# All pairs of a hybrid decoder layer's output projection by seven products

## The chip, the cores and the metric

The kernel runs on one core of a Trainium2 chip. The metric is the device time of one execution in microseconds (us); lower is better. A core has five engines that run side by side and meet at semaphores: TensorE (PE, matmuls into PSUM; its weight loads are shown as PEld), VectorE (DVE), ScalarE (ACT), GpSimd (POOL) and SyncE (SP), which here only issues DMAs. Each engine takes its instructions in order. A kernel's time is the median of several runs; one more execution was recorded by the hardware profiler, and all rows quoted here are of that one.

## The reference

One step of a decoder layer: a norm, a combined input projection, three groups of heads, and one output projection of width 1024.

```python
def _layer(x, conv_buf, buf_k, buf_v, mem_k, mem_v, ...):
    h = _rmsnorm(x, g_pre)
    z = h @ w_in                       # 1024 -> 2816 columns
    cb, cc, ch, cg, q, k, v, ag, mq, mg = _split_cols(z)
    out_a = silu(cg) * cb * conv3(cc * ch)              # 256 features
    out_b = silu(ag) * sliding_window_attention(q, k, v, sinks, window=128)   # 512
    out_c = silu(mg) * attention(mq, mem_k, mem_v)      # 256
    y = jnp.concatenate([out_a, out_b, out_c], axis=-1) @ w_out   # 1024 -> 1024
    return x + _rmsnorm(y, g_post), ...
```

It is computed for a prompt of 4096 tokens and for 8 sequences of 8 new tokens (the sample, 64 rows), in float32.

## The kernel before

**Precision and products.** Every float32 operand of a large matmul is split into a high and a low part in a reduced type (fp32r); a product is the sum of three matmuls, hi x hi, lo x hi and hi x lo. The split is one copy on ScalarE and one subtraction on VectorE. A 2 x 2 block product can be made from seven block products instead of eight, from sums and differences of the blocks of both operands. The input projection is made in this way but for the first two blocks of phase one.

**Stages.** `input_projection` runs through three phases over groups of columns of w_in. Each phase has eight blocks of 520 tokens, and each block seven products (eight plain ones in those two). Phase two (`ph == 1`) ends with q, k and v written to DRAM. Phase three has fewer columns, and carries the memory keys and the attention of the first 256 tokens beside it. Then comes the third stage, which the change is about: the attention and the output projection, 16 pairs of 128-token blocks.

**The output projection.** Blocks 0 to 5 (pairs 0 to 2) are plain: `Block.split` parts the gated features ("mix"), and `Block.run` makes two halves of 512 columns of eight k-tiles each, line 1639. From pair 3 on (`PLAIN_PAIRS = 3`) `Pair.run` makes a 2 x 2 block product: the two token blocks against the two halves of the columns, over feature tiles 0 to 3 only (two k-tiles per block of features). Feature tiles 4 to 7 are added with plain matmuls into the same PSUM banks. All its matmuls are made in the inner `product`, line 1750, one k-tile at a time; before each k-tile it calls what the list `starts` has for that step. A pair has 30 steps. Products with new=True begin a bank, others accumulate on it. The sums of features are made by GpSimd (`sums_of`, line 1695), their parts by ScalarE and VectorE (`lows`, lines 1678 and 1681). The five sums of weights are made by VectorE (`weight_sum`) during the plain pairs. All weight tiles stay in SBUF: pool `wa` has 21 slots of 4 KB a partition, pool `wt` six. A bank is read in parts: L1785 copies c12 to s3, L1787 adds c21 to s3 into s4, L1790 and L1793 subtract c12 and c21 from s4, L1759 copies a finished half, L1770 adds the last.

The order of the products before, with the number of k-tiles, is: c12 by a11 x T3 (2), c21 by a22 x T4 (2), c12 by rows0 x b22 (2), c21 by rows1 x b11 (2), then plain (8), c11 by diag x T1 (2), plain (2), c11 by down1 x T7 (2), plain (4), c22 by down0 x T6 (2), plain (4).

**Attention.** It runs one half (128 queries) at a time, ahead of the projection, in pieces that are hung on steps of the pair. `first_half` has transposes of the memory probabilities (L1368), window scores (L1333), and the products of the half before with the values (L1390, L1396, L1059); VectorE and ScalarE then mask, reduce and exponentiate (L1342, L1343, L1281, L1289), and the gates (L1255, L1407) multiply the results into mix. `memory_half` makes memory scores (L1355), `second_half` the window transposes (L1378) and the loads for the half after next. In a pair, the odd half's three pieces stand at steps 12, 16 and 19, the even half's at 24, 27 and 32, which is step 2 of the next pair.

**Who sets the order.** TensorE's order in the third stage is the program's (`manual_schedule`). Other engines' instructions are ordered by the scheduler from expected times, except those in `keep_in_program_order`. SP's DMAs are issued in such an order too, and one that waits holds all behind it. PSUM: two banks "z" for the projection, three pairs of banks for the attention.

Of the kernel before, what the change touches and what calls it, by code (L numbers as in the profile page):

```python
# [47 lines left out]
def f(ap):  # L48
    return ap.bitcast(F32)
# [3 lines left out]
def hybrid_layer(ctx: ExitStack, tc: tile.TileContext, a: dict):  # L53
# [834 lines left out]
    wo, wo_raw = [[None, None] for _ in range(KT)], {}  # L888

    def wo_load(j):  # L890
        h, k = divmod(j, KT)
        if 10 <= j < 14:

            if j % 2 == 0:
                third["raw"] = hxp.tile([P, KH, HW], F32, tag="hx", name=f"wor{j}").rearrange("p k n -> p (k n)")
            wo_raw[j] = third["raw"][:, 512 * (j % 2) : 512 * (j % 2) + 512]
        else:
            wo_raw[j] = third["work"].tile([P, 512], F32, tag="u", name=f"wor{j}")
        DMA.dma_start(wo_raw[j], a["w_out"][k][:, 512 * h : 512 * h + 512])

    def wo_split(j):
        h, k = divmod(j, KT)
        wo[k][h] = wa.tile([P, 2, 512], F32R, tag="w", name=f"wo{k}_{h}")
        w_split(wo[k][h], wo_raw.pop(j))
# [16 lines left out]
    def input_projection():  # L921
        for i, (ph, b, p) in enumerate(steps):
# [32 lines left out]
            if i > 0 and steps[i - 1][0] == 1 and steps[i - 1][1] == NBLK - 1:  # L955

                o = PRODUCTS[steps[i - 1][2]][0]
                for q in range(len(PHASES[2])):
# [5 lines left out]
                    else:  # L964
                        jobs.append(load)
                        pending.setdefault(i + 1, []).append(fill)
            if ph == 2 and b == last:
                for j in ((0, 1, 2), (3, 4), (5, 6, 7), (8, 9, 10, 11), (12, 13, 14, 15), (), ())[p]:
                    jobs.append(lambda j=j: wo_load(j))
                    pending.setdefault(i + (3 if j in (10, 11) else 2), []).append(lambda j=j: wo_split(j))  # L970
                if p == 1:
                    pending.setdefault(i + 1, []).append(gains_load)
                if p == 4:
                    jobs.append(blocks[0].split)
# [36 lines left out]
    def open_attention():  # L1011
# [14 lines left out]
        bp = {"k": att.enter_context(tc.tile_pool(name="keys", bufs=1)), "vT": att.enter_context(tc.tile_pool(name="vT", bufs=1))}  # L1026
# [41 lines left out]
    class Chunk:  # L1068


        def __init__(self, c):
            self.c, self.rds, self.q, self.ks = c, {}, [None, None], [None, None]
            self.t0 = NS + CT * c
            self.ts = slice(self.t0, self.t0 + CT)
# [6 lines left out]
        def load_all_keys(self):  # L1081

            self.kst = third["pre"].tile([P, 4, P + CT], F32R, tag="k", name="kst0")
# [581 lines left out]
    class Pair:  # L1665


        def __init__(self, c):
            self.c = c
# [461 lines left out]
```

## Time and profile before

| | |
|---|---|
| runs, median (lowest to highest) | 1519.56 us (1518.1 to 1525.04) |
| profiled execution, span | 1517.9 us |
| PE, DVE, ACT, POOL busy | 1500.6, 1199.3, 842.7, 392.7 us |
| matmuls, all | 11497 |
| first and last matmul of the plain blocks | 928.7 and 1042.6 us |
| matmuls of `Pair.run` | from 1042.8 us |
| DMA, whole span | 319.71 MB, mean 211 GB/s |

The profiled execution's own span is the time against which sums are made. Matmuls are pipelined: the duration of one includes the way through the array, so durations overlap, and the distance between two starts says what one costs. A row of groups gives a line, an engine, an operation, the tiles written and read, shapes, a count, and busy time and mean duration; behind the second bar stands idle time before it and what ended that. A row of the timeline begins with its start and its duration. In a row of waits stand total, number and longest.

### The profile page before, as it was taken

What the parts mean: (1) busy time and instruction counts of PE and PEld (TensorE: products, weight loads), DVE (VectorE), ACT (ScalarE), POOL (GpSimd) and SP (SyncE); (2) the same over time, 40 slices, a digit from 0 to 9 for tenths busy, and PEclk for the clock granted to TensorE, in tenths of its full rate; (3) what the DMA queues carried; (4) which work ended last, traced back from release to release, by engine and by line L of the source; (5) the groups of instructions that cost most, each with busy time, mean ns of one, the idle gap of its engine ahead of it and who ended that gap; (6) DMA issues with size and microseconds to landing.
All of it is one profiled execution on the core that took longest, in us unless ns stands there. A gap on an engine that the chain in (4) does not pass through costs nothing.

```text
span 1517.9 us, 30946 instructions
## 1 busy us (share of the span) xinstructions
PE 1500.6 (99%) x11497; PEld 1378.7 (91%) x11497; DVE 1199.3 (79%) x2089; ACT 842.7 (56%) x2066; POOL 392.7 (26%) x576
## 2 busy tenths in 40 slices
PE   9999999999999999999999999999999999999997
PEld 9999999999999999999999999788888788877875
DVE  6779888899988777897777768777877788878874
ACT  6676666475322222354454536666666666666652
POOL 0223222211300000000201301234455544455641
PEclk9999999999999999999999999999999999999999
DMA  9999999878855333578786697989755565666552
GB/s 258 157 265 221 289 294 271 264 246 298 211 183 183 128 116 125 180 235 292 227 265 238 208 307 252 282 238 238 201 168 157 160 164 162 176 174 169 153 201 70
DMA packets 217323, 319.71 MB, mean 211 GB/s; under 512 B 37398, under 2 KB 143382, under 8 KB 217142
## 3 DMA queue, kind: packets, MB, share of 16 engines
q1 hardware_dynamic: 196837, 273.54, 61.1%
q0 software_dynamic: 19616, 43.15, 10.5%
q8 instruction: 91, 1.49, 0.4%
q10 hardware_dynamic: 720, 1.05, 0.2%
q14 instruction: 59, 0.48, 0.1%
HBM read 208.50 MB, written 110.15 MB: 210 GB/s over the span
## 4 chain that ended last, share of the span: by engine, by line
PE 79%; DVE 8%; DMA 5%; ACT 4%; issue 2%; SPq 1%; POOL 0%; ACTq 0%; DVEq 0%; POOLq 0%
PE c L368 53%; PE y_c L1750 12%; PE y L1639 2%; PE ws L1333 2%; PE xt L1368 2%; ACT xp L1180 1%; DVE xr L1660 1%; DMA place<-in_xt 1%; PE wo L1059 1%; PE wo L1396 1%; DVE xmx L1169 1%; PE xs L1355 1%; DMA wr_3A<-in_w_in 1%; PE wt L1378 1%; DMA kst<-qd 1%
## 5 line engine op out<-in xcount | busy, mean ns | idle before, releaser
L375 DVE TENSOR_TENSOR z<-c,z 128x520 f32<-128x520 f32 (+1 forms) x308 | 194.3, 644 | 83.7 <-PE c L368 82.7
L1750 PE MATMUL y_c<-wo,pw 128*128 128x512 f32 (+1 forms) x636 | 158.9, 392 | 0.0
L1289 ACT ACTIVATE sm<-sm,wnm 128x128 f32<-128x128 f32 x256 | 99.4, 389 | 72.1 <-DVE wnm L1283 72.1
L1750 PEld LDWEIGHTS y_c<-wo,pw 128*128 128x128 f32 x636 | 114.0, 188 | 27.1 <-issue 3.7
L1192 POOL TENSOR_SCALAR xp<-xp,xrd 128x256 f32<-128x256 f32 x128 | 71.5, 575 | 191.2 <-DVE xrd L1186 186.7
L1180 ACT ACTIVATE xp<-xs,xnm 128x256 f32<-128x256 f32 x128 | 59.1, 473 | 31.5 <-DVE xnm L1170 22.9
L737 POOL CAST wmask<-negs 128x256 uint8<-128x256 f32 x1 | 1.2, 1162 | 266.7 <-DMA negs<-in_wmask 266.7
L1639 PE MATMUL y<-wo,mh 128*128 128x512 f32 x192 | 64.5, 398 | 0.2 <-ACT y L1648 0.2
L1312 POOL TENSOR_SCALAR_AFFINE_SELECT wpv<-wpt 128x512 f32<-128x512 f32 x62 | 56.8, 938 | 8.7 <-ACT wpt L1307 8.5
L1315 POOL TENSOR_SCALAR_AFFINE_SELECT wpt<-wpt 128x512 f32<-128x512 f32 x64 | 46.0, 737 | 38.6 <-ACT wpt L1307 38.2
L1333 PE MATMUL ws<-kst,q 128*128 128x256 f32 (+1 forms) x480 | 55.7, 297 | 0.0
L1343 DVE COPY_PREDICATED sm<-wmask,ws 128x512 f32<-128x512 uint8 x60 | 40.5, 729 | 19.0 <-ACT sm L1342 19.0
L1660 DVE SCALAR_TENSOR_TENSOR xr<-yn,yst,xr 128x1024 f32<-128x1024 f32 (+2 forms) x35 | 51.6, 1479 | 4.6 <-POOL yst L1655 4.5
L407 ACT CAST zh<-z 128x520 fp32r<-128x520 f32 x56 | 33.3, 624 | 35.3 <-DVE z L375 31.9
L276 ACT ACTIVATE nat<-nat 104x1024 f32<-104x1024 f32 x40 | 42.2, 1056 | 18.3 <-DMA nat<-in_x_p 18.3
L377 ACT COPY z<-c 128x520 f32<-128x520 f32 (+1 forms) x44 | 24.4, 554 | 49.3 <-PE c L368 45.0
L1333 PEld LDWEIGHTS ws<-kst,q 128*128 128x128 f32 (+1 forms) x480 | 46.4, 187 | 4.1
L1289 ACT ACTIVATION_READ_ACCUMULATOR sm<-sm,wnm 128x1 f32 x256 | 47.9, 187 | 0.0
L1297 DVE TENSOR_TENSOR sm<-sm,wrd 128x512 f32<-128x512 f32 x64 | 44.5, 695 | 1.1
L1750 PE MATMUL y_c<-wo,pc 128*128 128x512 f32 (+1 forms) x162 | 45.1, 400 | 0.0
L164 POOL DMA_DIRECT2D md<-th x48 | 26.2, 547 | 72.0 <-DVE th L425 59.5
L1639 PEld LDWEIGHTS y<-wo,mh 128*128 128x128 f32 x192 | 36.1, 188 | 8.9 <-issue 1.0
(1037 smaller groups left out, 5538.8 us busy)
## 6 DMA issues: line engine op xcount, KB each, us to landing
q<-qd SPq DMA_DIRECT2D x168, 128.0 KB
xr<-in_x_p SPq DMA_DIRECT2D x32, 512.0 KB
nat<-in_x_p SPq DMA_DIRECT2D x39, 416.0 KB
o_yp<-xr SPq DMA_DIRECT2D x31, 512.0 KB
kst<-qd SPq DMA_DIRECT2D x112, 128.0 KB
md<-th POOLq DMA_DIRECT2D x48, 260.0 KB, 6.4
qd<-zh SPq DMA_DIRECT2D x48, 260.0 KB
qd<-z SPq DMA_DIRECT2D x48, 260.0 KB
```

The costliest lines, as they stand in the source:

```text
L368: TE.matmul(bank[:, :HW], l, r, start=first and i == 0, stop=last and i == 3 * KH - 1)
L375: add = lambda dst, other: V.tensor_tensor(dst, c, other, op=ALU.add)
L1180: S.activation(p[:, i, :], s[:, i, :], AF.Exp, bias=nm[:, i : i + 1], scale=SCALE, accum_out=den[:, i : i + 1])
L1192: G.tensor_scalar(p[:, i, :], p[:, i, :], self.rds[h][:, i : i + 1], 0.5, op0=ALU.mult, op1=ALU.mult)
L1289: S.activation(sm[:, hh, :], sm[:, hh, :], AF.Exp, bias=nm[:, hh : hh + 1], scale=SCALE, accum_out=den[:, hh : hh + 1])
L1297: V.tensor_tensor(sm, sm, rd.unsqueeze(2).to_broadcast([P, 4, P]), op=ALU.mult)
L1312: G.affine_select(pv.rearrange("p (h q) -> p h q", h=4), p3, pattern=[[0, 4], [-1, P]], compare_op=ALU.is_gt, fill=0.0, base=0, channel_mu ...
L1315: G.affine_select(p3, p3, pattern=[[0, 4], [1, P]], compare_op=ALU.is_ge, fill=0.0, base=0, channel_multiplier=-1)
L1333: TE.matmul(out(kvh, col, bank), q(kvh, col, bank)[r], k(kvh, part)[r], start=first, stop=True, skip_group_check=not first, **place)
L1639: TE.matmul(acc, self.hl[l][:, k], wo[k][p][:, r], start=k + i == 0, stop=k + i == KT + 1)
L1660: x = V.scalar_tensor_tensor(self.xr[:m, cs], yn[:m, cs], st[:m, 3:4], self.xr[:m, cs], op0=ALU.mult, op1=ALU.add)
L1750: TE.matmul(acc, a[:, l, k], w[:, r, cs], start=first, stop=k == len(ws) - 1 and i == 2, skip_group_check=not new)
```

## The change

- All 16 pairs are made by `Pair.run`, and all eight feature tiles go into the 2 x 2 product: four k-tiles per product, seven products, 28 steps. `Block.split` and `Block.run` stay for the sample alone.
- The order becomes: c12 by a11 x T3, c12 by rows0 x b22, c21 by a22 x T4, c21 by rows1 x b11, c11 by diag x T1, c22 by down0 x T6, c11 by down1 x T7. In the last pair T7 stands before T6, and T6 is made in two halves of 256 columns after the sample.
- Weights: seven operands of four k-tiles. 21 of these tiles are made in phase two, blocks 1 to 6: raw tiles are loaded, GpSimd adds and subtracts, ScalarE copies, and the parts go to DRAM on GpSimd's queue. b22 and three tiles of b11 are split in phase three as before.
- 22 weight tiles stay in SBUF, and six (`STREAMED`: the fourth tile of each operand but b22) are loaded again in each pair, on SP's queue.
- Every operand of features takes one slot of `wa`: a11, rows0, a22, rows1, diag, down0, down1. They and the reloaded tiles share five slots; a slot is used for about ten steps.
- Keys: each half loads 128 tokens into a ring of three blocks, instead of 256 into a tile of its own.
- Places: the odd half's pieces at 11, 14, 18, the even half's at 22, 25 and 32 (step 4 of the next pair).

```diff
+    G0, G1 = (0, 1, 4, 5), (2, 3, 6, 7)
+    OUT_SUMS = {"T1": ((G1, 0), (G0, 1)), "T3": ((G1, 1), (G0, 1)), "T4": ((G0, 0), (G1, 0)), "T6": ((G1, 0), (G1, 1)),
+                "T7": ((G0, 0), (G0, 1)), "b11": ((G1, 0),), "b22": ((G0, 1),)}
+    STREAMED = (("T3", 3), ("T4", 3), ("b11", 3), ("T1", 3), ("T6", 3), ("T7", 3))
...
+    def out_sum(o, j):
+        x, y = out_raw.pop((o, j))
+        if o in WALKED:
+            G.tensor_tensor(x, x, y, op=ALU.subtract if o in ("T3", "T4") else ALU.add)
+        hi, lo = y.bitcast(F32R), x.bitcast(F32R)
+        S.copy(hi, x)
+        G.tensor_tensor(lo, x, f(hi), op=ALU.subtract)
+        G.dma_start(f(td[o, j][:, 0]), f(hi))
+        G.dma_start(f(td[o, j][:, 1]), f(lo))
+
+    out_sums_at = [(1, b, p) for b in range(1, NBLK - 1) for p in ((5, 6) if b < 4 else (1, 2, 3, 4, 5))]
...
+    def out_load(o, j, pool=None):
+        t = wo[o][j] = (pool or wa).tile([P, 2, 512], F32R, tag="w", name=f"wo{o}_{j}")
+        DMA.dma_start(f(t), f(td[o, j]))
...
-        wt = att.enter_context(tc.tile_pool(name="wt", bufs=6))
+        wt = att.enter_context(tc.tile_pool(name="wt", bufs=7))
...
         def load_keys(self, i):
...
+            at = (2 * self.c + i + 1) % 3 * P
+            self.fill_keys(G if self.c == 1 else DMA, third["ring"][:, :, at : at + P], self.t0 + i * P, P)
...
+        def lows(self, name, src):
+            self.ops[name] = t = wa.tile([P, 2, 512], F32R, tag="w", name=f"{name}{self.c}").rearrange("p a (b n) -> p a b n", n=P)
+            hi, lo = (t[:, i].rearrange("p (a c) n -> p a c n", a=2) for i in range(2))
+            S.copy(hi, src)
+            V.tensor_tensor(lo, src, f(hi), op=ALU.subtract)
...
+        def sum(self, name, x, y, op, raw=None):
+            def fn():
+                t = raw() if raw else sums["sum"].tile([P, 512], F32, tag="sum", name=f"r{name}{self.c}")
+                self.raws[name] = t = t.rearrange("p (a c n) -> p a c n", a=2, c=2)
+                G.tensor_tensor(t, self.part(*x), self.part(*y), op=op)
+            return fn
...
         def run(self, starts, sample=lambda: None):
...
+            def product(acc, name, o, new, cs=left_):
+                for j in range(4):
                     if cs.start == 0:
                         starts.get(at[0], lambda: None)()
                         at[0] += 1
+                    a_, w = self.ops[name], wo[o][j]
                     for i, (l, r) in enumerate(((0, 0), (1, 0), (0, 1))):
+                        TE.matmul(acc, a_[:, l, j], w[:, r, cs], start=new and j + i == 0, stop=j == 3 and i == 2, skip_group_check=not new)
...
+            c12 = psum("z", f"y{c}_c12")
+            product(c12, "a11", "T3", True)
+            tc.keep_in_program_order(S.copy(s3, c12))
+            product(c12, "rows0", "b22", False)
+            S.copy(half(0, 1), c12)
+            c21 = psum("z", f"y{c}_c21")
+            product(c21, "a22", "T4", True)
             V.tensor_tensor(s4, s3, c21, op=ALU.add)
+            V.tensor_tensor(half(0, 0), s4, c12, op=ALU.subtract)
+            product(c21, "rows1", "b11", False)
+            V.tensor_tensor(s3, s4, c21, op=ALU.subtract)
+            S.copy(half(1, 0), c21)
...
             c11 = psum("z", f"y{c}_c11")
+            product(c11, "diag", "T1", True)
             V.tensor_tensor(s3, s3, c11, op=ALU.add)
...
             if not last:
                 c22 = psum("z", f"y{c}_c22")
+                product(c22, "down0", "T6", True)
+                V.tensor_tensor(half(1, 1), c22, s3, op=ALU.add)
...
+                product(c11, "down1", "T7", False)
+                V.tensor_tensor(half(0, 0), c11, half(0, 0), op=ALU.add)
...
+    STEPS = 28
+    pairs = {c: Pair(c) for c in range(NCH)}
+    start_of = lambda c: STEPS * c
...
+    turns = lambda first, odd, even: {2: first} | {h: start_of((h - 3) // 2) + (odd if h % 2 else even) for h in range(3, 2 * NCH + 1)}
+    first_at, memory_at, second_at = turns(0, 11, 22), turns(3, 14, 25), turns(8, 18, STEPS + 4)
...
+    OP_AT = {"a11": (None, -7), "rows0": (-8, -3), "a22": (None, 1), "rows1": (0, 5), "diag": (6, 9), "down0": (8, 13), "down1": (11, 17)}
+    LOAD_AT = {"T3": -3, "T4": 1, "b11": 5, "T1": 13, "T6": 17, "T7": 21}
     for c, p in pairs.items():
         e = start_of(c)
+        for o, n in LOAD_AT.items():
+            if e + n > 0 and (o, c) != ("T4", 0):
+                at(e + n, lambda o=o: out_load(o, 3))
+        for name, (n, m) in OP_AT.items():
+            if c == 0 and name in ("a11", "rows0", "a22"):
+                continue
+            if n is not None:
+                at(e + n, lambda p=p, name=name: p.jobs()[name][0]())
+            at(e + m, lambda p=p, name=name: p.jobs()[name][1]())
...
+        if c > 0:
+            at(e + 3, lambda: left.pop(0)(True))
+            at(e + 6, lambda: left.pop(0)(True))
```

A pair of numbers in `OP_AT` is the step of GpSimd's sum and that of the split, counted from the pair's first step. `left` holds the ends of finished blocks: the addition to the input rows on VectorE (L1660) and the store on SP (L1663).

More of the change, by code (lines that the diff above doesn't have):

```diff
@@ L1780, in ends @@
                 left.append(lambda queued: b.finish(y[n], st[n], a["o_yp"][b.b * P : (b.b + 1) * P, :], queued, last and n == 1))
-            plain = lambda col, ks: [wo[k][col] for k in ks]
-            c12, c21 = psum("z", f"y{c}_c12"), psum("z", f"y{c}_c21")
-            product(c12, self.a11, t["T3"], True)
-            S.copy(s3, c12)
-            product(c21, self.a22, t["T4"], True)
-            V.tensor_tensor(s4, s3, c21, op=ALU.add)
-            product(c12, self.rows[0], b22, False)
```

380 lines of the change are left out of this document (124 added, 256 removed).

## The prediction

> **What bounds the kernel now.** I read the head of the page first, then busy time by stage, then the output projection's matmuls, then one stretch of the timeline around them.
>
> ```profile
> span 1517.9 us, 30946 instructions
> PE 1500.6 (99%) x11497; PEld 1378.7 (91%) x11497; DVE 1199.3 (79%) x2089; ACT 842.7 (56%) x2066; POOL 392.7 (26%) x576
> PEclk9999999999999999999999999999999999999999
> ...
> 300.00:400.00 100.00, 100.00 (x843) 99.83 (x842) 95.23 (x125) 61.07 (x105) 27.07 (x39) 1.00 0.81 243
> 500.00:600.00 100.00, 100.00 (x845) 100.00 (x844) 79.31 (x108) 28.65 (x34) 0.00 (x0) 1.00 0.38 132
> ...
> 929.00:1043.00 114.00, 112.84 (x751) 91.95 (x750) 87.97 (x208) 74.46 (x254) 37.97 (x59) 1.00 0.94 264
> 1043.00:1468.00 425.00, 422.92 (x2827) 340.07 (x2827) 337.80 (x757) 284.51 (x968) 212.46 (x290) 1.00 0.62 171
> ```
>
> A window row gives its length, then busy time of PE, PEld, DVE, ACT and POOL, the granted clock, the DMA share and GB/s. The last two rows are the third stage: 929 to 1043 the three plain pairs, 1043 to 1468 the pairs by products up to the last. PE is full in every row (422.92 of 425.0), at full clock, and DVE is next (337.80, 79%). So the time is PE's work plus PE's waits, and the question is how much of each the change takes and makes.
>
> **Matmuls removed.** These rows count those of the output projection.
>
> ```profile
> L1639 PE MATMUL y<-wo,mh x192: 387/389/501, 928.7 to 1042.6; 128*128 128x512 f32 x192
> ...
> L1639 PE MATMUL y<-wo,ml x96: 387/389/398, 929.0 to 1042.4; 128*128 128x512 f32 x96
> ...
> L1750 PE MATMUL y_c<-wo,pw x636: 279/389/504, 1049.8 to 1507.9; 128*128 128x512 f32 x153, 128*128 128x256 f32 x6
> ...
> L1750 PE MATMUL y_c<-wtT,pd x78: 387/389/398, 1059.2 to 1483.3; 128*128 128x512 f32 x78
> ```
>
> Six plain blocks have 288 (192 + 96), 96 a pair. A pair by products has 14 k-tiles in seven products and 16 plain ones, three matmuls each: 90. After the change every pair has seven products of four k-tiles: 84. That is 3 x 12 + 13 x 6 = 114 matmuls of 512 columns fewer. The 389 ns are not their price, since they overlap. The timeline gives it (start, duration, engine, line, count):
>
> ```profile
> 1253.18 2.25 PE L1750 MATMUL y_c<-wo,pw 128*128 128x512 f32 x9
> ...
> 1255.26 1.53 PE L1750 MATMUL y_c<-wtT,pa 128*128 128x512 f32 x6
> ...
> 1256.63 1.03 PE L1378 MATMUL wt<-ident,sm 128*128 128x128 f32 x8
> ...
> 1257.64 1.64 PE L1750 MATMUL y_c<-wtT,pa 128*128 128x512 f32 x6
> ...
> 1258.69 0.59 ACT L1785 COPY s<-y_c 128x512 f32<-128x512 f32 x1
> ...
> 1259.34 3.08 PE L1750 MATMUL y_c<-wo,pr 128*128 128x512 f32 x12
> ...
> 1262.26 2.98 PE L1750 MATMUL y_c<-wo,pw 128*128 128x512 f32 x12
> ...
> 1265.27 0.59 ACT L1759 COPY yn<-y_c 128x512 f32<-128x512 f32 x1 [3.33 <-PE y_c L1750]
> ```
>
> Nine in a row take 2.25, twelve 2.98 us; less the last one's 0.39 over the steps between starts that is 0.2325 and 0.235. At 0.233 the 114 are worth **-26.6 us**. This is the whole gain, 1.7% and not the 3% that 114 x 0.39 would suggest.
>
> **Waits that go.** Of the two runs "pa" the first goes into c12 and the second into c21; "pr" then goes on in c12, once ScalarE has copied c12 out (L1785, ending 1259.28). From 1257.64 six matmuls need 1.40, so "pr" could start at 1259.04 and starts at 1259.34: a wait of 0.30 a pair, 13 x 0.30 = -3.9 us. The plain stage's waits (114.0 - 112.84 = 1.2) I count as gone for 1.
>
> **Waits that come.** In the new order both sums of one bank follow each other: T3 then b22 into c12, T4 then b11 into c21, and the first must be read out before the second accumulates on it. Two boundaries of a pair's 28 steps (three matmuls, 0.70 us each) so lose the cover that the other bank's product gave.
>
> Step 4, c12: the even half's window transposes stand there now (second_half at STEPS + 4), eight of 1.03 us and two more. A reader starts when the last matmul has ended (1262.26 + 2.98 = 1265.24, copy at 1265.27) and takes 0.59: so the bank is free 0.16 + 0.03 + 0.59 + 0.06 = 0.84 after the nominal next start, under 1.03: the lower end is nothing. But ScalarE was late before too (a11's run ended at 1256.79, its copy began at 1258.69, 1.9 later, behind the memory exponentials); now that product ends later against them. If it were as late again, the wait would be 0.84 + 1.9 - 1.3 = 1.4, the upper end. I take the 0.30 of today, 16 x 0.30 = +4.8.
>
> Step 12, c21: nothing of the attention stands there. first_half of the odd half is at step 11, ahead of a22's last three matmuls. Today it stands at step 12, and the rows show what VectorE has in its queue just then:
>
> ```profile
> 1265.87 1.85 PE L1333 MATMUL ws<-kst,q 128*128 128x256 f32 x16
> ...
> 1267.70 1.07 ACT L1342 COPY sm<-ws 128x512 f32<-128x512 f32 x2
> ...
> 1267.82 0.69 DVE L1681 TENSOR_TENSOR pc<-yn,pc 128x512 fp32r<-128x512 f32 x1 [1.83 <-ACT pc L1678]
> ...
> 1268.43 1.34 DVE L1343 COPY_PREDICATED sm<-wmask,ws 128x512 f32<-128x512 uint8 x2
> ...
> 1269.15 1.04 PE L1059 MATMUL wo<-xp,mkv 128*64 128x128 f32 x16
> ...
> 1269.67 1.26 DVE L1281 TENSOR_REDUCE wmx<-sm 128x4 f32<-128x512 f32 x2
> ...
> 1270.13 1.66 PE L1750 MATMUL y_c<-wo,pw 128*128 128x512 f32 x6
> ...
> 1270.92 0.68 DVE L1255 TENSOR_TENSOR place<-place,wo 128x512 f32<-128x512 f32 x1
> ...
> 1271.66 0.41 DVE L1407 TENSOR_TENSOR place<-place,wo 128x256 f32<-128x256 f32 x1
> ```
>
> The projection resumes at 1270.13. Three matmuls on, at 1270.83, PE wants to write c21 again. The last of them starts at 1270.60 and ends at 1270.99, so s4 = s3 + c21 can start at 1271.02. VectorE, though, serves masks, maxima and both gates (L1255, L1407) first: they are ready earlier and earlier in the program. They end at 1272.07; then the add (0.68, as L1255) and a release of 0.06 (1259.28 to 1259.34): PE goes on at 1272.81, 1.98 late. The subtraction at 1267.82 will have gone, which lets the masks start up to 0.19 sooner, when the first score copy has ended (1267.70 + 1.07/2 = 1268.24 against 1268.43). So 1.8 to 2.0, and I take **1.9 us**. Lower end: the add ahead of the gates, 1271.02 + 0.68 + 0.06 - 1270.83 = 0.93. Upper end: a subtraction of 0.9 (rows below) in front as well, 2.8. Of these 1.9 follows the order that the rows show. It hits the 15 pairs that hold an odd half, and 0.93 the last pair, where no half runs: 15 x 1.9 + 0.9 = **+29.4 us**. Behind the waiting matmul all of PE is queued.
>
> **Work that is hidden.** For five of seven operands GpSimd now makes a raw sum of 512 columns, and ScalarE and VectorE split seven tiles instead of 5.5.
>
> ```profile
> L1695 POOL TENSOR_TENSOR yn<-place 128x512 f32<-128x512 f32 x6 | 8.7, 1457 | 0.0
> ...
> L1681 DVE TENSOR_TENSOR pw<-place,pw 128x512 fp32r<-128x512 f32 x12 | 10.8, 903 | 0.5
> ...
> L1776 DVE TENSOR_TENSOR yn<-yn,gpost 128x512 f32<-128x512 f32 x11 | 12.7, 1154 | 0.0
> ...
> L1770 DVE TENSOR_TENSOR yn<-y_c,s 128x512 f32<-128x512 f32 x12 | 8.2, 683 | 0.0
> ...
> L1678 ACT CAST pw<-place 128x512 fp32r<-128x512 f32 x12 | 8.1, 671 | 0.0
> ```
>
> Per pair: VectorE 1.5 x 0.90 = 1.4, ScalarE 1.5 x 0.67 = 1.0, GpSimd 2.5 x 1.46 = 3.6 us. Over the 12 pairs of 1043 to 1468 they now have 28.2, 23.7 and 17.7 of 35.4, so 29.6, 24.7 and 21.3 of some 36: no engine overtakes PE, and the price is nothing except in VectorE's queue at step 12. Two inputs in SBUF are slow beside GpSimd's work (1154 and 903 ns against 683 with one input in PSUM); the add on c21 is of the second kind.
>
> The Trainium skill ("SBUF — State Buffer", section "Who interferes with whom") says that a VectorE instruction with two SBUF inputs and a GpSimd instruction that reads SBUF block each other. The rows agree. By the page, all 3.6 us of new sums could be lost to VectorE, 33 of 36 us a pair, still under PE, so the sum stays.
>
> Phase two: 21 weight tiles at two GpSimd operations (1.46), one copy, two raw loads and two stores. GpSimd sleeps there (0.00 in 500 to 600) and DMA has 0.38; a block of 336 matmuls takes 40 us (845 in 100), and five tiles of 1 MB in it add some 125 GB/s. PE stayed at 100.00 with VectorE at 95.23 and DMA at 0.81 (300 to 400). Price nothing; without that cover, 42 GpSimd operations that each stretch a VectorE instruction by up to 0.47 (1154 - 683 ns) would be 20 us. The 16 splits of weights at the end of phase three fall to seven, off the path.
>
> Reloads: 6 x 512 KB a pair, less 512 KB for keys that are no longer read twice: 171 GB/s x 35.4 us = 6.1 MB becomes 8.7, 240 GB/s. At 171/0.62 = 276 GB/s per full share that is 0.87; the plain stage ran at 0.94 with 1.2 us of PE's waits. Nothing again, if each load is in time (rivals).
>
> **The sum**: -26.6 - 3.9 - 1.0 + 4.8 + 29.4 = +2.7 us on the profiled span: 1520.6. The runs' median of 1519.56 is 1.7 above the span, so **1522 us**.
>
> **Rivals.** (a) The scheduler puts the add ahead of the gates, wait 0.93: the step costs 16 x 0.93 = 14.9 in place of 29.4, **1507**. For: VectorE's order is not written out. Against: the gates are ready 0.8 us sooner. (b) No wait worth the name at either boundary, only the matmuls go: 1519.56 - 26.6 - 4.9 = **1488**. Against: the bank cannot be read and accumulated at once. (c) Diag's subtraction, which waits for a later GpSimd sum, stands ahead of the add: wait 2.8, 15 x 0.9 more, **1535**. For: GpSimd gets 3.6 us more work, and the sum for diag is queued behind the window masks. (d) The slower one: the fourth T3 tile comes late. Its slot is free when T6 ends (step 23) and its matmul is at step 3: seven steps and the memory scores, 4.9 + 1.1 = 6.0 us. SP issues in order, and stores stand in its way:
>
> ```profile
> SPq L1663 <- DVE xr L1660: 48.2, 12, 12.3
> ```
>
> Such a store holds SP 4.0 us on average. Behind one, with 1.9 us for 512 KB at 276 GB/s, its issue and a queue of other loads, the load lands after 6.0 us from there on; 1 to 2 us a pair more, **1537 to 1552**. Against: today's stores are not at that step. (e) The change does its work but phase two gives back 3 of those 20 us: 1525.
>
> **Chances.** Forecast (1517 to 1526) 0.34, (a) 0.22, (b) 0.13, (c) 0.12, (d) 0.16, (e) 0.03. A measurement of this kernel can tell 0.5% (7.6 us) from no change. Faster by more: (a) and (b), 0.35; within: the forecast and most of (e), 0.36; slower: (c), (d) and the rest, 0.29. From 1500 to 1540 leaves out (b) and the upper half of (d), 0.2. The likeliest case alone spans 1517 to 1526.
>
> **What would show it.** Per pair: 84 projection matmuls; PE idle at the start of b11's product, put down to VectorE's add on c21, near 1.9 us (0.9 in (a), 2.8 in (c)); 0 to 1.4 at b22's start, put down to ScalarE's copy; no wait of PE for a load of wo (else (d)); a pair's period near 36 us against 35.34 now (the next "pa" run after 1255.26 starts at 1290.60). Phase two should still show PE at 100. I am wrong if PE does not wait at step 12, or if it waits for weights.
>
> ```profile
> 1290.60 1.53 PE L1750 MATMUL y_c<-wtT,pa 128*128 128x512 f32 x6
> ```

## The result and the profile after

The kernel after takes **1637.2 us** (median of 4 runs, 1635.6 to 1640.2) against 1522.3 of the kernel before (4 runs, 1518.1 to 1525.4): a ratio of 1.076, 95% interval 1.073 to 1.079. I had forecast 1522, with a range from 1500 to 1540. The head of its page:

```profile
span 1634.9 us, 31287 instructions
...
PE 1536.2 (94%) x11377; PEld 1387.8 (85%) x11377; DVE 1236.4 (76%) x2090; ACT 866.3 (53%) x2092; POOL 554.6 (34%) x690
...
PEclk9999999999999999999999989999999999999997
```

TensorE has 120 matmuls fewer (108 of 512 columns and 12 of 256, worth the 114 of the prediction) and yet is busy 36 us longer, and the span grew by 117.0 us. Both together mean idle time and a slower clock. The windows say where (length, busy time of PE, PEld, DVE, ACT and POOL, granted clock, DMA share, GB/s):

```profile
500.00:600.00 100.00, 95.59 (x774) 94.57 (x773) 76.93 (x100) 32.62 (x44) 38.78 (x43) 0.97 0.62 219
943.00:1078.00 135.00, 114.91 (x701) 89.61 (x700) 88.58 (x201) 78.02 (x263) 57.57 (x70) 0.92 0.84 244
1078.00:1569.00 491.00, 440.80 (x2752) 341.05 (x2751) 358.74 (x756) 294.80 (x965) 262.60 (x302) 0.96 0.73 210
1569.00:1635.00 66.00, 47.97 (x238) 34.42 (x236) 31.43 (x71) 19.21 (x51) 14.65 (x18) 0.80 0.45 156
```

Phase two no longer keeps PE at 100, and in every part of the third stage PE idles and the clock is below 1. Measured from the first matmul of the output projection and the first of each pair:

| part | before, us | after, us | more |
|---|---|---|---|
| up to the first output matmul | 928.7 | 943.0 | 14.2 |
| first three pairs | 114.1 | 135.0 | 20.9 |
| next twelve pairs | 424.6 (35.38 each) | 491.5 (40.96 each) | 66.9 |
| last pair, sample block, ends | 50.5 | 65.4 | 15.0 |
| span | 1517.9 | 1634.9 | 117.0 |

Of the first row's 14.2 us, 11.7 arise in phase two: the input projection ends at 940.6 instead of 928.9, and the whole delay is there by 702. The rest is the window scores that now stand ahead of the first output matmul (1.9 us, and 0.5 of wait).

What PE waited for, summed over the run (engine, line, releaser; us, times, longest):

```profile
PE wo L1423 <- ACT xp L1402: 39.1, 13, 3.3
PE y_c L1742 <- DVE s L1765: 11.0, 12, 1.0
PE y_c L1742 <- ACT s L1760: 6.7, 12, 4.9
...
PE y_c L1742 <- ACT rows L1689: 3.6, 1, 3.6
```

The second row is the wait at step 12 that I had made the main cost: about 1 us a pair, not 1.9. The first row is a wait that I had not foreseen. L1423 is the odd half's products, L1402 ScalarE's copy of the transposed shares out of the one pair of banks "x" that the products need. The timeline of one pair:

```profile
1209.33 2.20 POOL L1342 TENSOR_SCALAR_AFFINE_SELECT wpv<-wpt 128x512 f32<-128x512 f32 x2
...
1209.95 1.04 PE L1401 MATMUL xt<-ident,xp 128*128 128x128 f32 x8
1210.74 1.86 PE L1365 MATMUL ws<-ring,q 128*128 128x256 f32 x16
...
1211.48 1.22 POOL L1345 TENSOR_SCALAR_AFFINE_SELECT wpt<-wpt 128x512 f32<-128x512 f32 x2
...
1212.67 1.26 POOL L1699 TENSOR_TENSOR rdiag<-place 128x512 f32<-128x512 f32 x1
1213.89 1.26 POOL L1699 TENSOR_TENSOR yn<-place 128x512 f32<-128x512 f32 x1
1213.97 0.62 ACT L1689 CAST diag<-rdiag 128x512 fp32r<-128x512 f32 x1 [5.27 <-POOL rdiag L1699]
1214.49 1.01 ACT L1402 COPY xp<-xt 128x1024 f32<-128x1024 f32 x1
...
1215.64 0.69 PE L1423 MATMUL wo<-wpv,vt 64*64 64x256 f32 x2 [3.04 <-ACT xp L1402]
```

Read it from the bottom. PE had its window scores issued by 1212.6 and idled 3.04 us for the copy L1402. The transposes that it copies ended at 1211.0, so the copy could have run then; but ScalarE takes its queue in order, and ahead of the copy stood the cast of diag, which had idled ScalarE for 5.27 us waiting for GpSimd's sum. That sum is a new one, and it stood behind the window masks (L1342, L1345), which end at 1212.7. The same masks are needed by the products, so without the cast PE would have gone on at about 1212.8.

The windows around that wait show a second loss:

```profile
1208.00:1212.60 4.60, 4.60 (x34) 3.87 (x32) 1.68 (x2) 0.59 (x1) 4.60 (x7) 1.00 0.88 275
1212.60:1215.60 3.00, 0.01 (x2) 0.00 (x0) 0.98 (x1) 1.63 (x3) 2.55 (x3) 1.00 0.70 237
1215.60:1219.10 3.50, 3.46 (x24) 1.98 (x26) 2.88 (x8) 1.34 (x5) 1.27 (x1) 0.51 0.77 184
1219.10:1220.70 1.60, 1.59 (x16) 0.94 (x13) 0.85 (x3) 1.33 (x9) 0.00 (x0) 1.00 0.85 262
```

After 3 us without a matmul the granted clock is half of full for 3.41 us (the record runs from 1215.65), which does 1.7 us less work. A twelfth of the regular stretch is such a window: one a pair, 12 x 3.413 = 40.96 us apart.

So a regular pair stands thus, in us: six matmuls fewer -1.40; the wait at step 4 0.32 for the 0.30 that went; step 12 +1.07; the odd half's products +3.1; the clock +1.7; the even half's products, whose masks come late, +0.8. That is +5.3 of the 5.57 measured; the rest is spread over starts of transposes. The 1.7 of the clock is worked out from its record and not from a run of its own.

### The profile page after: what moved, and what is told of

It reads as the page before. It is cut to its first block, busy times and chain, and to the rows that moved or that the text cites. A ratio compares the mean times of both kernels' runs of the same rounds, so it can differ in the third digit from the quotient of the medians.

```text
span 1634.9 us, 31287 instructions
## 1 busy us (share of the span) xinstructions
PE 1536.2 (94%) x11377; PEld 1387.8 (85%) x11377; DVE 1236.4 (76%) x2090; ACT 866.3 (53%) x2092; POOL 554.6 (34%) x690
## 4 chain that ended last, share of the span: by engine, by line
PE 66%; DVE 11%; POOL 10%; DMA 5%; issue 3%; ACT 3%; SPq 1%; DVEq 0%; ACTq 0%; POOLq 0%
PE c L368 43%; PE y_c L1742 9%; POOL xp L1222 3%; PE wo L1429 3%; PE wo L1423 2%; PE wo L1091 2%; POOL wpv L1342 2%; PE ws L1365 1%; POOL rdiag L1699 1%; DVE z L375 1%; DMA os1T<-in_w_out 1%; PE xs L1388 1%; DMA woT<-tdT 1%; POOL yn L1752 1%; POOL wpt L1345 1%
## 5 line engine op out<-in xcount | busy, mean ns | idle before, releaser
L1742 PE MATMUL y_c<-wob,rows 128*128 128x512 f32 x384 | 104.3, 416 | 22.1 <-DVE s L1765 11.0
L1742 PEld LDWEIGHTS y_c<-wob,rows 128*128 128x128 f32 x384 | 72.3, 198 | 45.9 <-DVE s L1765 16.4
L1742 PE MATMUL y_c<-woT,a 128*128 128x512 f32 x384 | 100.8, 404 | 6.5 <-DVE a L1690 3.7
L1742 PE MATMUL y_c<-woT,down 128*128 128x512 f32 (+1 forms) x396 | 100.7, 396 | 0.6 <-DVE down L1690 0.3
L1742 PEld LDWEIGHTS y_c<-woT,a 128*128 128x128 f32 x384 | 72.3, 192 | 24.5 <-DVE a L1690 4.5
L1742 PEld LDWEIGHTS y_c<-woT,down 128*128 128x128 f32 x396 | 71.4, 191 | 18.2 <-issue 3.0
L909 POOL TENSOR_TENSOR os0T<-os0T,os1T 128x512 f32<-128x512 f32 x20 | 25.9, 1297 | 133.1 <-DMA os1T<-in_w_out 131.2
L1210 ACT ACTIVATE xp<-xs,xnm 128x256 f32<-128x256 f32 x128 | 58.9, 471 | 19.3 <-DVE xnm L1200 18.5
L1423 PE MATMUL wo<-wpv,vt 64*64 64x256 f32 x120 | 25.1, 498 | 42.5 <-ACT xp L1402 39.1
L1342 POOL TENSOR_SCALAR_AFFINE_SELECT wpv<-wpt 128x512 f32<-128x512 f32 x62 | 56.7, 935 | 13.3 <-ACT wpt L1337 13.3
L1365 PE MATMUL ws<-ring,q 128*128 128x256 f32 (+1 forms) x480 | 55.9, 298 | 0.5 <-DVE z L375 0.5
L1742 PE MATMUL y_c<-woT,diag 128*128 128x512 f32 x192 | 51.4, 403 | 0.0
L1365 PEld LDWEIGHTS ws<-ring,q 128*128 128x128 f32 (+1 forms) x480 | 46.5, 187 | 4.8 <-DVE z L375 0.7
```

The source lines that it names most:

```text
L1210: S.activation(p[:, i, :], s[:, i, :], AF.Exp, bias=nm[:, i : i + 1], scale=SCALE, accum_out=den[:, i : i + 1])
L1342: G.affine_select(pv.rearrange("p (h q) -> p h q", h=4), p3, pattern=[[0, 4], [-1, P]], compare_op=ALU.is_gt, fill=0.0, base=0, channel_mu ...
L1365: TE.matmul(out(kvh, col, bank), q(kvh, col, bank)[r], k(kvh, part)[r], start=first, stop=True, skip_group_check=not first, **place)
L1423: TE.matmul(o[cs, 1 - n], v[rs, cs], p3[rs, :, 64 - 64 * n : 128 - 64 * n], start=True, stop=False, tile_position=(64 - 64 * n, 64 * kvh))
L1742: TE.matmul(acc, a_[:, l, j], w[:, r, cs], start=new and j + i == 0, stop=j == 3 and i == 2, skip_group_check=not new)
```

## The experiments

My theory after this reading: the sums that GpSimd now makes are late, and the casts that wait for them hold ScalarE's queue in front of copies that PE needs. The rivals: GpSimd is overloaded whoever waits for it; the bank waits at steps 4 and 12 are the loss; the reloads are; phase two is a matter of its own. Each time below is of one execution beside one of the kernel before, which took 1519 to 1525 us. "Period" is the time from the first T3 matmul of a pair to that of the next, in the middle of the third stage.

### The cast of diag behind the copy

```
-    OP_AT = {... "diag": (6, 9), ...}
+    OP_AT = {... "diag": (6, 13), ...}
```

> The kernel after, with one number changed: the split of the diagonal sum (ScalarE's cast and VectorE's subtraction) is issued at step 13 of a pair instead of step 9, so that in ScalarE's order it stands behind the copy of the odd half's transposes instead of ahead of it. GpSimd's own order and load hardly change. Theory (ScalarE's queue is held by a cast that waits for a late GpSimd sum): the 3.0 to 3.3 us in which TensorE waits at the odd half's products shrink to under 0.6, since the masks end at about the time the window scores end; the half-clock window of each pair goes with it; the pair period falls from 41.0 to about 36, the time by 14 x 5.0 = 70 to about 1567 us. Rival (GpSimd is simply too loaded, whoever waits for it): the wait moves to the masks or to the diagonal product and the period stays above 39.5, time over 1615. Rival (the waits at the accumulating banks are the loss): no change, 1630 to 1640.

1597.3 us, period 37.4 (37.8 on the mean of the twelve pairs). PE's waits between 1000 and 1500 us:

```profile
PE y_c L1742 <- DVE s L1765: 15.4, 12, 1.4
PE y_c L1742 <- ACT yn L1769: 5.2, 12, 0.5
PE y_c L1742 <- ACT s L1760: 4.7, 12, 0.6
```

The wait at the products is gone, and between 989 and 1541 us no half-clock window is left. GpSimd's load and order are nearly unchanged, so ScalarE's queue is what it was. But I had expected 1567: the pair gained 3.1 us on the mean and not 5.0, since three bank waits grew as PE came earlier (step 12 to 1.3 idle), and the first pair got longer, from 53.3 to 57.5.

### No sums at all

```
-                t = raw() if raw else sums["sum"].tile(...)
-                self.raws[name] = t = t.rearrange(...)
-                G.tensor_tensor(t, self.part(*x), self.part(*y), op=op)
+                self.raws[name] = self.part(*x)
```

> The kernel after without the five GpSimd sums of a pair: each sum's first term stands for the sum (the output isn't the reference's), while the casts stand in ScalarE's order where they stood, diag's ahead of the transposes' copy. Theory (the cast holds the queue only because GpSimd's sum is late): the wait at the odd half's products and the half-clock windows go, and with them the late masks of the even half; the waits at steps 4 and 12 stay; period about 36.5 or less, time 1575 or less. Rival (the added casts and subtractions load ScalarE and VectorE too much whatever GpSimd does): period 38 or more, time over 1590.

1563.1 us, period 36.3, as the theory had it but for one point: the even half's masks stay late. The 64-row products (L1423) still take 1.9 us a pair, against 1.2 in the kernel before, so the sums aren't the cause of that term. ScalarE's order is that of the kernel after, the cast of diag ahead of the copy; it only has nothing to wait for.

```profile
PE y_c L1740 <- DVE s L1763: 17.6, 13, 1.8
PE y_c L1740 <- ACT s L1758: 2.1, 12, 0.4
```

Of the waits that come back in every pair only the two at the banks are left, the one at step 12 now 1.35 us idle on average, 1.6 from start to start. The difference of the spans, 1634.9 - 1561.4 = **73.5 us, is what the five sums of a pair cost** in this order, of 117.0 in all.

### No reloads

```
     def out_load(o, j, pool=None):
+        if j == 3:
+            wo[o][3] = wo[o][2]
+            return
```

> The kernel after without the fourth tile of six of the seven weight matrices: wherever the fourth tile of a matrix would be used, its third is used again, so that none is loaded in a pair (the output isn't the reference's). Theory (the reloads are in time and cost nothing): 1632 to 1640 us, period 41.0. Rival (the six loads of a pair take the queues or the memory from others, or TensorE waits for them): period under 40, time 1620 or less.

1658.0 us: slower by 20, though the third stage now moves some 120 instead of 210 GB/s. Neither theory nor rival had this. The timeline of ScalarE says why:

```profile
1269.61 0.62 ACT L1692 CAST down<-yn 128x512 fp32r<-128x512 f32 x1 [5.14 <-POOL yn L1702]
1270.13 0.61 ACT L1692 CAST down<-rdown 128x512 fp32r<-128x512 f32 x1
1270.65 1.00 ACT L1405 COPY xp<-xt 128x1024 f32<-128x1024 f32 x1
```

Without the loads to wait for, the scheduler put both casts of "down" ahead of the copy as well, and with them two more sums behind the masks. PE's wait grew to 5.6 us on average (67.3 us in 12 pairs) and the half-clock window to 6.83. A change that touches no cast moved the time by moving casts, so this run doesn't give the price of the reloads. In the kernel after PE waits only 0.3 us for them in all. But two stretches got shorter without them: the first pair took 44.3 us instead of 53.3, and the last with the ends 52.1 instead of 65.4. Whether that is the loads, the slots that they share with the operands, or again the order of the casts, no run shows.

### The bank waits

The odd half at step 12 instead of 11, so that it stands between the two products on c21:

```
-    first_at, memory_at, second_at = turns(0, 11, 22), turns(3, 14, 25), ...
+    first_at, memory_at, second_at = turns(0, 12, 22), turns(3, 15, 25), ...
```

> The kernel after, with the odd half's first part at step 12 instead of 11 and its memory part at 15 instead of 14, so that the half stands between the last matmul of c21's first product and the product that accumulates on it; VectorE's read of c21 then has the half as its cover. Theory: the 1.07 us wait at step 12 goes; the wait at the odd half's products shortens by the one step (0.7 us) by which the half comes later and stays at about 2.4, still long enough for a half-clock window; period about 39.2, time about 1612 us. Rival (the bank wait is the main loss and the clock with it): period near 37, time 1580 or less. Rival (VectorE reaches the read only behind the half's masks and maxima, as forecast): a wait near 1 us remains, 1625 to 1635.

1647.3 us. The waits at steps 4 and 12 went (1.1 us left in 12 pairs), but the casts still held the copy, and now longer: 3.4 us a pair at the products. And the memory transposes (L1401) now waited for GpSimd, 1.25 us a pair.

```profile
PE wo L1423 <- ACT xp L1402: 41.1, 12, 3.7
PE xt L1401 <- POOL xp L1222: 15.0, 22, 1.1
...
1224.15 0.62 ACT L1689 CAST diag<-rdiag 128x512 fp32r<-128x512 f32 x1 [3.57 <-POOL rdiag L1699]
...
1225.83 0.43 PE L1423 MATMUL wo<-wpv,vt 64*64 64x256 f32 x2 [3.63 <-ACT xp L1402]
```

Taking the bank waits away thus gains nothing while the casts hold the copy. The later split of diag and the half at 12 together, with the three casts pinned behind the copy (a pinned instruction keeps its place in program order among the pinned ones):

> The kernel after with the casts of diag, down0 and down1 kept behind the copy of the odd half's transposes (split of diag at step 13, casts pinned), and the odd half at step 12 with its memory part at 15, the order of the products as in the kernel after. Against the run with the later split alone (1597 us, period 37.5) and the run with the half at 12 alone (1647 us): theory (the half at 12 covers the bank wait of step 12, and was slower only because the casts held ScalarE's queue): the 1.48 us wait goes, period about 36.0, time about 1576 us. Rival (the cover is paid back where the diagonal's parts come one step later than needed): period 37 or more, time over 1590.

1634.0 us, period 39.4 and later 41.0: the rival. Step 12's wait is gone, and in its place PE waits for diag's parts, which now come one step later than needed, and for the bank of c21 (1.2 us a pair), whose copy stands behind them, and 0.9 us a pair for the window masks. With the split of diag put between the copies of the window scores and the exponentials, and phase two's copies by GpSimd:

```
             sms...                                       # window_probabilities
+            between()
             dens = [self.window_exps(...) ...]
```

> As the run before it, but the split of diag stands between the copies of the window scores and the exponentials of the odd half, where ScalarE waits 2.1 us for VectorE anyway, and phase two's rounded copies are made by GpSimd. Theory: the parts of diag are ready before step 16, period 36.0 or less; phase two gives 8 us; time about 1565 us. Rival (GpSimd's sum of diag, behind the masks, is late there too and now holds the exponentials): period 37 or more, time over 1580.

1587.3 us, period 36.8 and 38.0 in turn, no half-clock window between 973 and 1460. Better by 50 than the kernel after, but short of 1565: PE waits for the masks, and 0.9 us for the weights of the window (DVE L1327) at the next transposes, and one pair near the end (the fourteenth) took 49.0.

The other way to take the bank waits away is the order of the products, c21's first product between the two on c12:

```
             product(c12, "a11", "T3", True)
+            c21 = psum("z", f"y{c}_c21")
+            product(c21, "a22", "T4", True)
+            V.tensor_tensor(s4, s3, c21, op=ALU.add)
             product(c12, "rows0", "b22", False)
```

> The kernel after with the casts of diag, down0 and down1 kept behind the copy of the odd half's transposes (the split of diag at step 13, the three casts pinned in program order) and with the second and third product exchanged: c12 by T3, c21 by T4, c12 by b22, c21 by b11, so that four steps stand between the two products on each bank; the parts of a22 are made at step -3 and those of rows0 at 1. Against the run with the later split alone (1597 us, period 37.5, waits of 1.48 at step 12 and 0.3 to 0.7 at step 4): theory (both bank waits are cover that the order of products took away): both go, period about 35.5, the first pair 4 us shorter, time about 1565 us. Rival (the waits move on to the next use of the two banks, at diag and down0): period 36.5 or more, time over 1580.

1616.4 us, period 39.2. The rival again:

```profile
PE y_c L1744 <- DVE yn L1768: 8.9, 11, 0.8
PE wo L1423 <- POOL wpt L1345: 8.1, 22, 0.9
PE y_c L1744 <- DVE diag L1692: 7.7, 12, 0.6
PE y_c L1744 <- ACT yn L1771: 7.4, 12, 0.6
PE y_c L1744 <- DMA woT<-tdT: 6.4, 9, 1.3
```

Two long waits became five short ones: at the next use of each bank, at the next operand, at the masks and at a load. There are two banks for four accumulators: whatever is read out later frees its bank later. The order of the products isn't all of it, though. The run also moved the sum of rows0 from step -8 to -4 and that of rows1 from 0 to 2, nearer to the odd half's masks, and it left T4's load at step 1 while its product came four steps earlier; the load waited for in the regular pairs is T4's each time. What the order costs alone is not shown.

### Phase two

```
-        S.copy(hi, x)
+        G.tensor_copy(hi, x)
```

The lead was ScalarE's waits of the kernel after between 400 and 600 us:

```profile
ACT os1T L911 <- POOL os0T L909: 46.5, 13, 7.3
...
ACT os1T L911 <- DMA os0T<-in_w_out: 6.4, 1, 6.4
```

> The kernel after, with phase two's rounded copies of the weight sums made by GpSimd instead of ScalarE, so that GpSimd adds, copies and subtracts in a row and ScalarE's queue holds nothing of the weight sums. GpSimd does 28 operations of about 1 us more than before. Theory (in phase two too ScalarE's queue was held by copies that waited for a GpSimd sum or a load): phase two ends at 929 instead of 940.6, no TensorE wait for hi or lo parts; time 12 lower, about 1625 us. Rival (GpSimd's arithmetic itself slows VectorE beside it): the loss stays or grows, 1635 to 1645.

1628.9 us, 8.3 less; the input projection (the expectation calls it the end of phase two) ends at 933.1 where it ended at 940.6, and at 928.9 before. GpSimd does more there than in the kernel after, and PE idles less:

```profile
500.00:600.00 100.00, 99.23 (x834) 98.82 (x834) 85.68 (x107) 29.07 (x35) 56.64 (x55) 1.00 0.68 235
```

So of phase two's 11.7 us some 8 were ScalarE's queue once more; 4 stayed. These are single runs, and they scatter: the input projection ended between 939.5 and 945.1 in the eight runs with ScalarE's copies, and between 929.8 and 935.8 in the seven with GpSimd's. Added to the exchanged products:

> As the run before it, and phase two's rounded copies of the weight sums made by GpSimd instead of ScalarE. Theory (phase two and the third stage add up): 8 us under the run before it, as the copies alone gave 8 on the kernel after. Rival (a third stage that starts earlier waits for its loads): less than 4.

1603.5 us, 12.9 under the run without it, more than the 8 expected: there the input projection had ended at 945.1, the latest, here at 929.8, the earliest of the changed kernels.

### The clock

> The kernel after with 12 needless matmuls of 128x512 put into the wait of each odd half, between the window scores and the products (they add to c21, so the output isn't the reference's). 12 x 0.233 = 2.8 us of the 3.0 to 3.3 us wait are filled. Theory (the half-clock window of each pair follows from TensorE's idle time, and costs 1.7 us a pair of its own): the half-clock windows of the steady pairs vanish, the wait for the transposes' copy remains as a few tenths of a us, period about 39.3, time about 1613 us. Rival (the half-clock window has another cause): the windows and the period of 41.0 remain, 1635 us or more.

1681.1 us: it does not answer its question. The needless matmuls moved VectorE's order too. Its add on c21 fell behind the gates and the first of the window's weights, and PE waited 4.1 us a pair at step 12 instead, with the half-clock window behind that:

```profile
PE y_c L1742 <- DVE s L1766: 45.0, 11, 4.2
```

The clock's own price is therefore read from its records, not shown by a run of its own.

### What the change is worth with free sums

The run without sums, with the odd half at 12 and phase two's copies by GpSimd:

> As the run without the five sums of a pair (1563 us, period 36.3, a wait of 1.6 at step 12 left; the output isn't the reference's), with the odd half at step 12, its memory part at 15 and its transposes at 19, and phase two's rounded copies by GpSimd. It asks what the change would be worth if its sums were free. Theory (what is left is the bank wait of step 12 and phase two): 14 x 1.6 = 22 and 8 us less, about 1533 us, period 34.7; still above the 1520 of the kernel before, because the first pair (53 us) and the last (56 us) stay. Rival (the later half is paid for elsewhere): period 35.7 or more, time over 1545.

1542.2 us, period 35.1, between the two:

```profile
PE wo L1423 <- POOL wpt L1345: 2.6, 13, 0.3
...
PE y_c L1740 <- ACT s L1758: 1.2, 7, 0.2
```

Hardly a wait is left in the regular pairs, and they are 0.3 us shorter than before the change. An output product's matmuls take 19.99 us of a pair against 21.56 before, start to start: the gain is there, 1.57 us. But the 64-row matmuls of the products take 2.03 instead of 1.22 (late masks) and the two transposes ahead of step 4 with what follows 0.55 instead of 0.14. And it starts 6.5 us later, the first three pairs take 125.3 against 114.1 and the end 56.3 against 50.5. Even with sums that cost nothing this order would be some 20 us slower than the kernel before: 22.6 against the profiled span above (1540.5 and 1517.9), 18.2 against the execution beside it (1542.2 and 1524.0).

### The sums respread

All five sums made, at other places: rows1's at -3, diag's at 3 in the free half of the second output tile, down1's at 13, a gain on VectorE instead of GpSimd, with the parts of the runs above that helped, and GpSimd's sums pinned in program order.

```
+    OP_AT = {"rows0": (-8, -5), "rows1": (-3, 6), "diag": (3, 9), "down1": (13, 17), ...}
-                gained(0, 0, G)
+                gained(0, 0)
```

> The whole change, all sums made, put where the runs say: rows1's sum at step -3 instead of 0 and split at 6; diag's sum at step 3 in the free half of the pair's second output tile instead of behind rows1's in the one shared buffer; down1's sum at 13, so that one sum at most stands ahead of the masks; the first block's last gain on VectorE instead of GpSimd; the casts of diag, down0 and down1 pinned behind the copy of the transposes, diag's between the copies of the window scores and the exponentials; the odd half at 12, memory at 15, its transposes at 19; phase two's rounded copies by GpSimd. Theory (order, not load, made the loss): period 36.0 or less, time about 1555 us. Rival (GpSimd's five sums are too much for the stretch ahead of the odd half in any order): period 37 or more, time over 1575.

1605.7 us, periods of 38 and 40. Neither theory nor rival had the cause, which is the first row:

```profile
PE y_c L1745 <- DMA woT<-tdT: 22.6, 18, 2.8
PE wo L1424 <- POOL wpt L1345: 3.5, 13, 0.4
```

In the regular pairs GpSimd is waited for no more than 0.4 us at a time, but the fourth tile of T3 is late in every regular pair (18.5 of the 22.6 us), and that of T1 in six (4.1). T3's load stands on SP's queue behind query loads that wait for the memory scores. That tile one step earlier:

> As the run with the sums respread (1606 us, period 38 and 40 in turn), with the fourth tile of T3 loaded at step -4 instead of -3, ahead of the query loads that wait for the memory scores on SP's queue, and rows0 split at -3. Theory (order, not load, made the loss): the waits for the tile go (22.6 us in 18 waits), the sums cost little beyond the run without them (35.1): period 36.0 or less, time about 1560 us. Rival (GpSimd's sums are too much ahead of the odd half in any order): masks or parts are waited for again, period 37 or more, time over 1575.

1595.7 us. T3's tile is in time, and now T1's is late, by up to 2.4 us:

```profile
PE y_c L1745 <- DMA woT<-tdT: 14.9, 12, 2.4
PE wo L1424 <- POOL wpt L1345: 4.7, 10, 0.7
```

Its load stands behind that of the next mix, which waits for down1's later sum (SP waits 36.8 us for it in nine pairs). Three tiles earlier:

> As the run before it (1596 us, period 37.3 to 39.4), with the fourth tiles of T1, T6 and T7 loaded at steps 11, 16 and 20 instead of 13, 17 and 21, so that T1's stands ahead of the load of the next mix on SP's queue. Theory (order, not load, made the loss): the 14.9 us of waits for the tiles go, period 36.5 or less, time about 1570 us. Rival (each late sum shows as another wait, in whatever place): period 37 or more, time over 1585.

1577.6 us, the best of the versions that compute everything; period 37.5, no half-clock window between 1017 and 1570.

```profile
PE wo L1424 <- POOL wpt L1345: 9.4, 22, 0.7
PE xs L1389 <- issue: 6.4, 11, 0.6
PE y_c L1745 <- ACT yn L1772: 4.7, 11, 0.4
```

The tiles are in time and the masks are waited for in both halves. (An idle time put down to "issue" is one for which the profile shows nothing that was waited for.) Places and order were worth 60 us in all, phase two's 8 among them; the last 2.4 us a pair over the 35.1 without sums stayed in every order tried. No version beat the kernel before.

## Why the prediction was wrong

**The step that failed** is "Work that is hidden": "no engine overtakes PE, and the price is nothing except in VectorE's queue at step 12". I added GpSimd's 3.6 us a pair to its busy time, found 21.3 of 36 and called it cover. The loads were added up rightly: VectorE, ScalarE and GpSimd have 29.9, 24.6 and 21.9 us in a regular pair of the kernel after, against 29.6, 24.7 and 21.3. The sums have room in a pair, but not where they stood: ahead of the odd half GpSimd works without a break from 1202.6 to 1215.2 (4.60 of 4.60 us in the window row from 1208), and the sum of diag is the last but one in it, from 1212.67 to 1213.93. What held PE was not VectorE's queue but ScalarE's: its cast idled for 5.27 us with a copy for PE behind it. The price is 73.5 us (the run without sums), of which moving one cast gave back 39.

**Rival (c)** had the late sum in it ("the sum for diag is queued behind the window masks") and followed it to the wrong queue. The split of an operand is a cast and a subtraction; I asked what is behind the subtraction on VectorE and not what is behind the cast on ScalarE.

**Matmuls removed**: right. 1.57 us a regular pair in the run without waits, against 1.40 and a part of the 0.30.

**Step 12**: the mechanism was right, the term too large. The add stands behind both gates:

```profile
1219.85 0.69 DVE L1285 TENSOR_TENSOR mix<-mix,wo 128x512 f32<-128x512 f32 x1 [1.06 <-PE wo L1091]
...
1220.53 0.41 DVE L1440 TENSOR_TENSOR mix<-mix,wo 128x256 f32<-128x256 f32 x1
1220.86 0.68 DVE L1765 TENSOR_TENSOR s<-s,y_c 128x512 f32<-128x512 f32 x1
...
1221.60 1.66 PE L1742 MATMUL y_c<-wob,rows 128*128 128x512 f32 x6 [0.90 <-DVE s L1765]
```

but it cost 1.07 us from start to start and not 1.9, because PE itself came to step 12 late, held at the products and slowed by the clock. Where that hold was gone it cost 1.5 to 1.6, still under 1.9.

**Step 4**: 0.32 in the regular pairs, as taken. In the first pair it was 4.9, beyond my upper end of 1.4: there the copy of c12 stands behind the exponentials of the window and of the memory.

**Phase two**: "Price nothing" was wrong by 11.7 us. That this lies inside the 20 that I had set without cover is luck, since the mechanism was another: not GpSimd's instructions stretching VectorE's, but ScalarE's copies waiting for a sum or a load in front of the parts of the next product.

**Reloads**: right for this kernel as far as PE's own wait goes, 0.3 us in all, and rival (d) did not come; that the first and the last pair are shorter without them I had not looked for. In the first two respread versions (d) did come, at up to 2.8 and 2.4 us, by the mechanism named, SP in order behind something that waits; but what waited there were loads of queries and of mix, not the stores that I had named.

**What had no term at all**: the granted clock, 1.7 us a pair; the first three pairs, 20.9; the last, 15.0. Most of the 20.9 is not the sums: in the first pair PE waits 4.9, 3.6 and 2.4 us and 13.7 us run at half clock, and without the sums that pair takes 53.3 us as well. The last is not explained by a run. In the kernel after 26.7 us of it are at half clock, 17.1 of them in one piece, against 5.9 before; half of the difference, 10.4 us, is an estimate of the clock's part of the 15.0. It is 56 us long with the sums left out, 52.1 without the reloads, and in the three respread versions 60.9, 65.8 and 50.3. What starts it stays open.

## What to carry over

When work is moved onto an idle engine, follow each result to the instruction that waits for it, and list what is queued behind that instruction on its own engine: an in-order queue passes a wait on to work that has nothing to do with it. Cover is a question of the place, not of the share; look at the engine's busy stretch just ahead of the need. And when a hold is removed, name the next one before counting the gain: here each of three cures gave back a part of its gain to the next bank, operand or load.

## What the runs showed of the hardware

The half-clock stretches begin on a fixed grid. In the kernel after, all their starts differ by whole multiples of 3.413 us, from 423.8 to 1632.1, and the regular pairs stay locked on to it at twelve windows each. Other runs do so at other whole numbers: thirteen a pair, 44.37 us, in most pairs without the reloads and with the needless matmuls, and 23 in two pairs with the sums respread. In all 16 traces, between 1000 and 1500 us, every full-clock window of the grid in which PE idled for 1.72 us or more (76 windows, in 13 of the traces) was followed by one at half clock. With 1.60 or less it nearly always stayed at full clock; the exceptions, idle for 1.04 to 1.37 us, were in the runs with the half at 12 and the casts pinned (seven) and with diag split inside the half (one), and I have no cause for them. The Trainium skill ("TensorE: Matmul & The Clock Gate", section "What's actually happening") gives a free-running window of 3413 ns, which these traces agree with, and a fall to half clock after at least one idle window; here half a window's idling was enough, so a wait of 2 us can cost 3.7.
